# Norms' 1/sqrt chains moved from GpSimd to VectorE, with squares and normalised rows made in halves

## The chip, the core and the metric

The kernel runs on one core of one Trainium2 chip. The metric is the device time of one execution in microseconds (us). TensorE (PE) multiplies matrices, VectorE (DVE) and ScalarE (ACT) do elementwise work, GpSimd (POOL) did the small chains that the change is about, and SyncE (SP) issues the DMAs. Each engine works through its own queue in order; engines wait for one another at semaphores.

## The reference

Two layers, each of three sub-layers on `x` of 256 rows by 1024 columns, in float32:

```python
for l in range(DEPTH):
    x = x + 0.5 * gate(0) * _swiglu(norm_mod(x, 0), w_ffn_up[l, 0], w_ffn_down[l, 0])
    x = x + gate(1) * _mixer(norm_mod(x, 1), w_in[l], ...)
    x = x + 0.5 * gate(2) * _swiglu(norm_mod(x, 2), w_ffn_up[l, 1], w_ffn_down[l, 1])
```

`norm_mod` divides each row by the root of its mean square (plus 1e-6), scales it by `g_norm * (1 + scale)` and adds `shift`. Shift, scale and gate come from the condition vector `c` through the large matrix `w_ada`. `_swiglu` is an FFN of width 2816. The mixer projects the rows once and runs an RG-LRU, a stick-breaking attention and a forgetting attention on parts of the columns. Each part's output is divided by its own root mean square before the last projection.

## The kernel before

The rows lie in two tiles of 128, `x0` and `x1` (index `t`), which stay in SBUF. All weights stream through a ring of six buffers (`raw`, 512 KB each). Each weight tile is split into two float32r parts: ScalarE casts it to `H` (L248), VectorE subtracts to get `L` (L249), and TensorE makes three products (rows' high part with `H` and with `L`, rows' low part with `H`). The `w_ada` tiles come through the same ring and are read by VectorE alone (L290 for shift and scale, L313 for the gates).

Between two sub-layers stands a norm, once for each row tile. There are five such boundaries: **B1** first FFN to first mixer, **B2** first mixer to its second FFN, **B3** from layer 1 to layer 2, **B4** first FFN of layer 2 to its mixer, **B5** that mixer to the last FFN. At each, for `x0` and then for `x1`:

- `residual` (L441, L442, VectorE) adds the gated result to `x`, half by half.
- `norm_sq` (ScalarE, `junk`) squares the row and sums it into `ss`. Before, one instruction did it, except for `x1` after an FFN, where two halves were added up on GpSimd (L397, `v`).
- `rsqrt` finds the inverse root by an integer guess and two Newton steps: `ny` (L356), `na` (L360), `ny` (L361), `na`, `ny`, five dependent instructions on 128x1. They ran on GpSimd.
- `norm_xn` (L404, ScalarE) scales the row into `xn`.
- `norm_out` transposes `xn` on TensorE (L415, `tp`), applies scale and shift (`hf`, half on ScalarE L423, half on VectorE L425), and splits into `hTh` (L428, L430) and `hTl` (L431), which the next sub-layer's matmuls read.

While `x1`'s chain runs, TensorE works on the next sub-layer with `x0`: 48 matmuls of 512 columns. The mixer has the same `rsqrt` on 128x2 in `group` for its two attention outputs (`f` and `s`), between `gj` (L842) and `yn` (L848), whose transposes are `ty` (L850). The output projection's matmuls are `wo`. At the very start the two norms (L918) have their squares on VectorE; of their chains, that of `x0` ran on GpSimd and that of `x1` on VectorE. GpSimd otherwise only clears the gates' accumulators (`acc`, L308).

The tile framework decides where each instruction stands in its engine's queue: it follows estimates of when operands will be there, and the explicit limits in the code (`tc.issue_after`, `pending`). So an operation that moves to another engine also changes what stands around it.

Of the kernel before, what the change touches and what calls it, by code (L numbers as in the profile page):

```python
# [12 lines left out]
I32 = mybir.dt.int32  # L13
AF = mybir.ActivationFunctionType
ALU = mybir.AluOpType
# [4 lines left out]
D = 1024  # L20
# [6 lines left out]
EPS = 1e-6  # L27
# [67 lines left out]
def trunk_kernel(ctx: ExitStack, tc: tile.TileContext, x, c, wst, ada, par, cst, row, bgate, wg, out):  # L95
    nc = tc.nc
# [13 lines left out]
    def W4(shape, dt=F32, name="w4"):  # L110
        return w4.tile(shape, dt, tag="w4", name=name)

    def W2(shape, dt=F32, name="w2"):
        return w2.tile(shape, dt, tag="w2", name=name)

    def SM(shape, dt=F32, name="sm"):
        return sm.tile(shape, dt, tag="sm", name=name)
# [4 lines left out]
    def PD(shape, name):  # L122
        return psd.tile(shape, F32, tag="d", name=name)

    def PT(shape, name):
        return pst.tile(shape, F32, tag="t", name=name)

    V, A, T, S = nc.vector, nc.scalar, nc.tensor, nc.sync
# [4 lines left out]
    xt = [x_t[:, 0:D] for x_t in xe]  # L133
# [34 lines left out]
    def R(name):  # L168
        o, n = ROW[name]
        return r_sb[:, o:o + n]  # L170
# [8 lines left out]
    for n in range(2):  # L179
        q = slice(n * 512, (n + 1) * 512)  # L180
# [71 lines left out]
    def unit(key):  # L252
        if key not in live:
            raw = rawp.tile([128, 1024], F32, tag="raw", name="raw")
            S.dma_start(out=raw, in_=wst[W_UNITS[key]])
            live[key] = split(raw)
        return live[key]

    def mm3(o, xh, xl, wh, wl, first, last):
        T.matmul(o, lhsT=xh, rhs=wh, start=first, stop=False)  # L260
        T.matmul(o, lhsT=xh, rhs=wl, start=False, stop=False)  # L261
        return T.matmul(o, lhsT=xl, rhs=wh, start=False, stop=last)  # L262
# [87 lines left out]
            ada_step(1)  # L350


    def rsqrt(v, n, name, E=nc.gpsimd):
        y = SM([128, n], name=name + "y")
        a = SM([128, n], name=name + "a")
        E.tensor_scalar(out=y.bitcast(I32), in0=v.bitcast(I32), scalar1=-0.5, scalar2=float(0x5F1FFFF9),  # L356
                        op0=ALU.mult, op1=ALU.add)
        for c in (-2.38924456, -3.0 / NEWTON ** 2):
            if n == 1:
                E.tensor_scalar(out=a, in0=y, scalar1=v, scalar2=y, op0=ALU.mult, op1=ALU.mult)  # L360
                E.tensor_scalar(out=y, in0=a, scalar1=c, scalar2=y, op0=ALU.add, op1=ALU.mult)  # L361
            else:
                E.tensor_tensor(out=a, in0=y, in1=y, op=ALU.mult)
                E.tensor_tensor(out=a, in0=a, in1=v, op=ALU.mult)
                E.tensor_scalar(out=a, in0=a, scalar1=c, scalar2=None, op0=ALU.add)
                E.tensor_tensor(out=y, in0=a, in1=y, op=ALU.mult)
        return y


# [12 lines left out]
    xn_t, r_t = {}, {}  # L382

    def norm_in(t):
        norm_sq(t)
        norm_xn(t)

    def norm_sq(t, parts=1):
        n = D // parts
        ss = SM([128, parts], name="ss")  # L390
        for i in range(parts):
            q = slice(i * n, (i + 1) * n + i // (parts - 1) if parts > 1 else D + 1)
            junk = W2([128, D + 1], BF16, name="junk")
            A.activation(junk[:, q], xe[t][:, q], AF.Square, scale=1.0 / 32, accum_out=ss[:, i:i + 1])
        if parts == 2:
            v = SM([128, 1], name="v")
            nc.gpsimd.tensor_tensor(out=v, in0=ss[:, 0:1], in1=ss[:, 1:2], op=ALU.add)  # L397
        else:
            v = ss
        r_t[t] = rsqrt(v, 1, "n")  # L400

    def norm_xn(t):
        xn_t[t] = W4([128, D], name="xn")
        A.activation(xn_t[t], xt[t], AF.Copy, scale=r_t[t])  # L404

    def norm_out(l, j, t):
        ada_until(ada_ss, (l, j, KT - 1, 1))
# [27 lines left out]
    def residual(l, j, t, o, each=lambda t, q: None):  # L435
        ada_until(ada_gate, (l, j, KT - 1))
        g = gate_t[l, j]
        for n in range(2):
            q = slice(n * 512, (n + 1) * 512)
            tmp = W2([128, 512], name="tmp")  # L440
            V.tensor_tensor(out=tmp, in0=o[n], in1=g[:, q], op=ALU.mult)  # L441
            V.tensor_tensor(out=xt[t][:, q], in0=xt[t][:, q], in1=tmp, op=ALU.add)  # L442
            each(t, q)
        if t == NT - 1:
            gate_free[j % 2] = True
# [24 lines left out]
    def ffn(l, s, after, pre={}):  # L470
# [66 lines left out]
        def down(j, t):  # L537
            if j == 0:
                dn[t] = [PD([128, 512], name="dn") for _ in range(2)]
            w = [unit(("dn", l, s, j, i)) for i in range(2)]  # L540

            order = [(i, n) for i in range(2) for n in range(2)]
            for i, n in sorted(order, key=lambda p: p[1]) if j == NCH - 1 else order:
                q = slice(n * 512, (n + 1) * 512)
                mm3(dn[t][n], *gT[j, i, t], w[i][0][:, q], w[i][1][:, q],
                    j == 0 and i == 0, j == NCH - 1 and i == 1)
            if j == NCH - 1:
                if after is None:
                    residual(l, j3, t, dn[t], lambda t, q: S.dma_start(out=out[t * 128:(t + 1) * 128, q], in_=xt[t][:, q]))
                    return  # L550
                residual(l, j3, t, dn[t])
                norm_sq(t, 1 + t)
                if t == 1:
                    norm_xn(1)
                    pending.append(lambda: after[1](1))
# [11 lines left out]
        a, b = NCH - 2, NCH - 1  # L567
# [14 lines left out]
    def mixer(l, after):  # L582
# [41 lines left out]
        if True:  # L624
            for f2, hf in enumerate(halves):
                for f in (2 * f2, 2 * f2 + 1):
                    A.activation(u[:, f, :], xT[:, f, 3:3 + SEQ], AF.Identity,
                                 scale=cw[:, 3 * 4 + f:3 * 4 + f + 1], bias=cbias[:, f:f + 1])
                    for tap in (2, 1, 0):
                        V.scalar_tensor_tensor(out=u[:, f, :], in0=xT[:, f, tap:tap + SEQ],  # L630
                                               scalar=cw[:, tap * 4 + f:tap * 4 + f + 1], in1=u[:, f, :],
                                               op0=ALU.mult, op1=ALU.add)
# [13 lines left out]
        for t in range(NT):  # L646
            o = proj(FX, t)
            if t == 1:
# [8 lines left out]
                for t in range(NT):  # L657
# [14 lines left out]
                            in1=r8.unsqueeze(2).to_broadcast([128, 8, HD]), op=ALU.mult)  # L672
            for i in range(2):
                V.tensor_tensor(out=qa[t][:, 4 * i:4 * i + 4, 0:HD], in0=qa[t][:, 4 * i:4 * i + 4, 0:HD],
                                in1=R(f"gqk{l}")[:, i * HD:(i + 1) * HD].unsqueeze(1).to_broadcast([128, 4, HD]),
                                op=ALU.mult)
# [29 lines left out]
        for f2, hf in enumerate(halves):  # L706
# [7 lines left out]
            for f in (2 * f2, 2 * f2 + 1):  # L714
                V.tensor_tensor_scan(out=hs[:, f, :], data0=rg[:, f, :], data1=ig[:, f, :], initial=0.0,
                                     op0=ALU.mult, op1=ALU.add)
# [87 lines left out]
        def split(f0, n, src):  # L804
            for i in range(n):
                g = gm[:, f0 + i:f0 + i + 1]
                yh, yl = hTh[:, :, f0 + i, :], hTl[:, :, f0 + i, :]
                y = src[:, i, :].rearrange("p (t q) -> p t q", t=NT)
                A.activation(yh, y, AF.Copy, scale=g)
                V.scalar_tensor_tensor(out=yl, in0=y, scalar=g, in1=yh.bitcast(F32),  # L810
                                       op0=ALU.mult, op1=ALU.subtract)


        for t in range(NT):
# [3 lines left out]
            q = slice(t * 128, (t + 1) * 128)  # L818
# [19 lines left out]
        def group(name, f0, src):  # L838
            s2g = SM([128, 2], name="gs" + name)
            junk = W2([128, 256], name="gj")  # L840
            for t in range(NT):
                A.activation(junk, src[t], AF.Square, accum_out=s2g[:, t:t + 1])  # L842
            nc.gpsimd.tensor_scalar(out=s2g, in0=s2g, scalar1=1.0 / 256, scalar2=EPS, op0=ALU.mult, op1=ALU.add)
            rs = rsqrt(s2g, 2, "g" + name)
            yn = W2([128, 2, 256], name="yn")
            tp = PT([128, 2, SEQ], name="ty")
            for t in range(NT):
                V.tensor_scalar(out=yn[:, t, :], in0=src[t], scalar1=rs[:, t:t + 1], scalar2=RS, op0=ALU.mult, op1=ALU.mult)  # L848
                for i in range(2):
                    T.transpose(tp[:, i, t * 128:(t + 1) * 128], yn[:, t, i * 128:(i + 1) * 128], ident)  # L850
            split(f0, 2, tp)
# [5 lines left out]
        def values(y, products):  # L857

            with ExitStack() as behind:
                for i, (t, h, w, v) in enumerate(products):  # L860
                    mul = T.matmul(y[:, t, h, :], lhsT=w, rhs=v, start=i == 0, stop=True, skip_group_check=True)
                    if i == 0:
# [8 lines left out]
                        in1=rin.unsqueeze(2).to_broadcast([128, 8, HD]), op=ALU.mult)  # L871
# [36 lines left out]
    def norm(l, j):  # L908
        return norm_in, lambda t: norm_out(l, j, t)
# [4 lines left out]
    for t in range(NT):  # L914
        ss = SM([128, 1], name="ss")
        junk = W2([128, D + 1], BF16, name="junk")
        x1 = xe[t][:, 0:D + 1]
        V.scalar_tensor_tensor(out=junk, in0=x1, scalar=1.0 / D, in1=x1, op0=ALU.mult, op1=ALU.mult, accum_out=ss)  # L918
        r_t[t] = rsqrt(ss, 1, "n", V if t == 1 else nc.gpsimd)
        norm_xn(t)  # L920
    xnT = [W4([128, NT, 4, 128], name="xnT") for _ in range(2)]
    for g in range(2):
# [7 lines left out]
    for k in range(KT):  # L930
        for v in range(2):
# [3 lines left out]
                        scalar2=S_t[0, 0][:, k:k + 1], op0=ALU.mult, op1=ALU.add)  # L935
# [117 lines left out]
```

## Time and profile before

| | us |
|---|---|
| median of three runs | 1032.69 (1031.07 to 1036.15) |
| the profiled execution | 1031.17 |
| its span, first to last instruction | 1029.4 |
| VectorE busy | 759.9 (74%) |
| ScalarE busy | 538.1 (52%) |
| GpSimd busy | 53.3 (5%), 108 instructions |

The page gives the busy time of each engine, then the chain of work that ended last, followed back from the last instruction, then the costliest groups. The trace behind it gives the instructions in order of time: start, duration, engine, line, `out<-in`, shapes, and in square brackets how long the engine had been idle and what ended that. Ends of matmuls are modelled, and one that overlaps the next shows a longer duration than its spacing: back-to-back 512-column matmuls start 0.23 us apart at the full clock.

### The profile page before, as it was taken

What the parts mean: (1) busy time and instruction counts of PE and PEld (TensorE: products, weight loads), DVE (VectorE), ACT (ScalarE), POOL (GpSimd) and SP (SyncE); (2) the same over time, 40 slices, a digit from 0 to 9 for tenths busy, and PEclk for the clock granted to TensorE, in tenths of its full rate; (3) what the DMA queues carried; (4) which work ended last, traced back from release to release, by engine and by line L of the source; (5) the groups of instructions that cost most, each with busy time, mean ns of one, the idle gap of its engine ahead of it and who ended that gap; (6) DMA issues with size and microseconds to landing.
All of it is one profiled execution on the core that took longest, in us unless ns stands there. A gap on an engine that the chain in (4) does not pass through costs nothing.

```text
span 1029.4 us, 15807 instructions
## 1 busy us (share of the span) xinstructions
PE 994.3 (97%) x6038; PEld 871.8 (85%) x6038; DVE 759.9 (74%) x1107; ACT 538.1 (52%) x855; POOL 53.3 (5%) x108
## 2 busy tenths in 40 slices
PE   5999999989999899999999999999999989999998
PEld 4999999868787799999878999997777778999996
DVE  7988978769786898888569888665677559745452
ACT  5373534458774444354454455455679454635340
POOL 1000000120011200000020000001100120000000
PEclk9999999989999999999999999999999999999999
DMA  8989998757473699999539999853542328755511
GB/s 307 362 308 315 332 332 312 268 207 255 155 252 117 241 362 336 335 331 328 194 124 340 342 334 335 304 191 137 173 175 83 103 86 324 266 203 171 198 63 41
DMA packets 68922, 248.10 MB, mean 241 GB/s; under 512 B 7783, under 2 KB 8423, under 8 KB 68846
## 3 DMA queue, kind: packets, MB, share of 16 engines
q1 hardware_dynamic: 68846, 247.10, 68.2%
q8 instruction: 47, 0.77, 0.3%
q14 instruction: 29, 0.24, 0.1%
HBM read 246.02 MB, written 1.05 MB: 240 GB/s over the span
## 4 chain that ended last, share of the span: by engine, by line
PE 83%; ACT 6%; POOL 4%; DVE 3%; issue 2%; DMA 1%; SPq 0%; DVEq 0%; POOLq 0%; ACTq 0%
PE up L467 38%; PE dn L260 8%; PE dn L262 8%; PE dn L261 8%; PE up L271 5%; PE pj L271 5%; PE up L273 3%; PE pj L273 2%; ACT H L248 2%; POOL na L360 1%; PE wo L260 1%; PE wo L261 1%; PE wo L262 1%; POOL ny L361 1%; PE tp L415 1%
## 5 line engine op out<-in xcount | busy, mean ns | idle before, releaser
L249 DVE TENSOR_TENSOR L<-raw,H 128x1024 fp32r<-128x1024 f32 x320 | 380.5, 1221 | 72.6 <-ACT H L248 71.8
L248 ACT CAST H<-raw 128x1024 fp32r<-128x1024 f32 x320 | 328.1, 1051 | 84.5 <-PE up L467 35.0
L467 PE MATMUL up<-hTh,H 128*128 128x256 f32 x1088 | 211.0, 282 | 3.7 <-ACT H L248 3.7
L467 PE MATMUL up<-hTl,H 128*128 128x256 f32 x1088 | 211.9, 283 | 0.0
L467 PE MATMUL up<-hTh,L 128*128 128x256 f32 x1088 | 211.3, 282 | 0.0
L467 PEld LDWEIGHTS up<-hTh,H 128*128 128x128 f32 x1088 | 169.2, 189 | 9.9 <-ACT H L248 4.1
L467 PEld LDWEIGHTS up<-hTl,H 128*128 128x128 f32 x1088 | 165.1, 189 | 0.0
L467 PEld LDWEIGHTS up<-hTh,L 128*128 128x128 f32 x1088 | 164.4, 189 | 0.0
L459 ACT ACTIVATE sg<-up 128x256 f32<-128x256 f32 x88 | 33.7, 383 | 223.9 <-PE up L467 183.6
L260 PE MATMUL dn<-H,gh 128*128 128x512 f32 x352 | 141.1, 401 | 1.6 <-ACT gh L532 1.6
L262 PE MATMUL dn<-H,gl 128*128 128x512 f32 x352 | 140.0, 399 | 0.0
L261 PE MATMUL dn<-L,gh 128*128 128x512 f32 x352 | 139.7, 397 | 0.0
L290 DVE SCALAR_TENSOR_TENSOR raw<-raw,cb 128x1024 f32<-128x1024 f32 x96 | 114.0, 1220 | 2.1 <-DMA raw<-in_ada 2.1
L262 PEld LDWEIGHTS dn<-H,gl 128*128 128x128 f32 x352 | 66.6, 189 | 15.8 <-DVE gl L533 0.5
L260 PEld LDWEIGHTS dn<-H,gh 128*128 128x128 f32 x352 | 66.7, 189 | 15.2 <-ACT gh L532 3.0
L261 PEld LDWEIGHTS dn<-L,gh 128*128 128x128 f32 x352 | 66.9, 190 | 12.8
L516 DVE TENSOR_TENSOR sg<-sg,up 128x256 f32<-128x256 f32 x68 | 28.5, 419 | 66.0 <-ACT sg L459 65.7
L271 PE MATMUL pj<-H,hTh 128*128 128x512 f32 x160 | 66.2, 414 | 0.0
L273 PE MATMUL pj<-H,hTl 128*128 128x512 f32 x160 | 65.9, 412 | 0.0
L271 PE MATMUL up<-H,hTh 128*128 128x512 f32 x160 | 64.2, 401 | 0.4 <-DVE hTh L428 0.4
L271 PE MATMUL pj<-L,hTh 128*128 128x512 f32 x160 | 64.5, 403 | 0.0
L271 PE MATMUL up<-L,hTh 128*128 128x512 f32 x160 | 63.1, 395 | 0.0
(249 smaller groups left out, 1101.5 us busy)
## 6 DMA issues: line engine op xcount, KB each, us to landing
raw<-in_wst SPq DMA_DIRECT2D x320, 512.0 KB, 5.2
raw<-in_ada SPq DMA_DIRECT2D x144, 512.0 KB, 5.3
x<-in_x SPq DMA_DIRECT2D x2, 512.0 KB, 3.7
wgt<-in_wg SPq DMA_DIRECT2D x2, 512.0 KB
out_x<-x SPq DMA_DIRECT2D x4, 256.0 KB
once<-in_cst SPq DMA_DIRECT2D x1, 192.0 KB
p_sb<-in_par SPq DMA_DIRECT2D x1, 148.0 KB, 5.4
r_sb<-in_row SPq DMA_DIRECT2D x1, 132.0 KB, 6.1
```

Source lines behind the costliest of these rows:

```text
L248: A.copy(h, raw)
L249: V.tensor_tensor(out=lo, in0=raw, in1=h.bitcast(F32), op=ALU.subtract)
L260: T.matmul(o, lhsT=xh, rhs=wh, start=first, stop=False)
L261: T.matmul(o, lhsT=xh, rhs=wl, start=False, stop=False)
L262: return T.matmul(o, lhsT=xl, rhs=wh, start=False, stop=last)
L271: T.matmul(o, lhsT=hh[:, k, :], rhs=part, start=k == 0 and i == 0, stop=False)
L273: mul = T.matmul(o, lhsT=hl[:, k, :], rhs=w(k)[0], start=False, stop=k == KT - 1)
L290: V.scalar_tensor_tensor(out=raw, in0=raw, scalar=1.0, in1=cb, op0=ALU.mult, op1=ALU.mult, accum_out=st[:, v, k:k + 1])
L360: E.tensor_scalar(out=a, in0=y, scalar1=v, scalar2=y, op0=ALU.mult, op1=ALU.mult)
L459: used.append(A.activation(*a, **k))
L467: return T.matmul(o[:, v], lhsT=w[:, q:q + 128], rhs=(hTh, hTl)[h][:, :, k, :], start=opens, stop=True, skip_group_check=True)
L516: V.tensor_tensor(out=sg, in0=sg, in1=o[:, 1], op=ALU.mult)
```

## The change

All `rsqrt` chains run on VectorE, as do the sum of the two halves' squares (`v`) and the scaling ahead of the mixer's chains (L843). For 128x2 the last two of four operations of a Newton step are one `scalar_tensor_tensor`. Squares are always made in two halves (512 and 513 columns), and `xn` in two halves of 512. Lines 394 and 397 are now 393 and 396.

```diff
-    def rsqrt(v, n, name, E=nc.gpsimd):
+    def rsqrt(v, n, name):
...
-        E.tensor_scalar(out=y.bitcast(I32), in0=v.bitcast(I32), scalar1=-0.5, scalar2=float(0x5F1FFFF9),
+        V.tensor_scalar(out=y.bitcast(I32), in0=v.bitcast(I32), scalar1=-0.5, scalar2=float(0x5F1FFFF9),
                         op0=ALU.mult, op1=ALU.add)
         for c in (-2.38924456, -3.0 / NEWTON ** 2):
             if n == 1:
-                E.tensor_scalar(out=a, in0=y, scalar1=v, scalar2=y, op0=ALU.mult, op1=ALU.mult)
-                E.tensor_scalar(out=y, in0=a, scalar1=c, scalar2=y, op0=ALU.add, op1=ALU.mult)
+                V.tensor_scalar(out=a, in0=y, scalar1=v, scalar2=y, op0=ALU.mult, op1=ALU.mult)
+                V.tensor_scalar(out=y, in0=a, scalar1=c, scalar2=y, op0=ALU.add, op1=ALU.mult)
             else:
-                E.tensor_tensor(out=a, in0=y, in1=y, op=ALU.mult)
-                E.tensor_tensor(out=a, in0=a, in1=v, op=ALU.mult)
-                E.tensor_scalar(out=a, in0=a, scalar1=c, scalar2=None, op0=ALU.add)
-                E.tensor_tensor(out=y, in0=a, in1=y, op=ALU.mult)
+                V.tensor_tensor(out=a, in0=y, in1=y, op=ALU.mult)
+                V.tensor_tensor(out=a, in0=a, in1=v, op=ALU.mult)
+                V.scalar_tensor_tensor(out=y, in0=a, scalar=c, in1=y, op0=ALU.add, op1=ALU.mult)
...
     def norm_in(t):
-        norm_sq(t)
+        norm_sq(t, 2)
...
-            nc.gpsimd.tensor_tensor(out=v, in0=ss[:, 0:1], in1=ss[:, 1:2], op=ALU.add)
+            V.tensor_tensor(out=v, in0=ss[:, 0:1], in1=ss[:, 1:2], op=ALU.add)
...
-        A.activation(xn_t[t], xt[t], AF.Copy, scale=r_t[t])
+        for q in (slice(0, D // 2), slice(D // 2, D)):
+            A.activation(xn_t[t][:, q], xt[t][:, q], AF.Copy, scale=r_t[t])
...
-                norm_sq(t, 1 + t)
+                norm_sq(t, 2)
...
-            nc.gpsimd.tensor_scalar(out=s2g, in0=s2g, scalar1=1.0 / 256, scalar2=EPS, op0=ALU.mult, op1=ALU.add)
+            V.tensor_scalar(out=s2g, in0=s2g, scalar1=1.0 / 256, scalar2=EPS, op0=ALU.mult, op1=ALU.add)
...
-        r_t[t] = rsqrt(ss, 1, "n", V if t == 1 else nc.gpsimd)
+        r_t[t] = rsqrt(ss, 1, "n")
```

The queues around the moved instructions differ at every boundary. At B1, ScalarE's queue from `x0`'s squares (`x_88`) to its normalised row, where L248 is the weight cast, L459 the SiLU of the last up-projection and L532 a cast that the down-projection waits for; before:

```order
L248 CAST H<-raw 128x1024 x2
L394 ACTIVATE junk,ss<-x_88 128x1025
L248 CAST H<-raw 128x1024
L459 ACTIVATE sg<-up 128x256
L404 ACTIVATE xn<-x_88,ny 128x1024
L454 ACT_TABLE_LOAD
L532 CAST gh<-tg 128x256
```

and now:

```order
L248 CAST H<-raw 128x1024
L393 ACTIVATE junk,ss<-x_88 128x512
L393 ACTIVATE junk,ss<-x_88 128x513
L248 CAST H<-raw 128x1024 x2
L459 ACTIVATE sg<-up 128x256
L454 ACT_TABLE_LOAD
L404 ACTIVATE xn<-x_88,ny 128x512 x2
L532 CAST gh<-tg 128x256
```

The squares stand one weight cast earlier, and the table load stands ahead of the normalised row, no longer between it and `gh`.

VectorE's queue at B1 from the end of `x1`'s residual (`x_89`) on, before:

```order
L442 TENSOR_TENSOR x_89<-x_89,tmp 128x512 x2
L249 TENSOR_TENSOR L<-raw,H 128x1024 x3
L604 MEMSET xT 128x4x3
L249 TENSOR_TENSOR L<-raw,H 128x1024 x2
L425 TENSOR_SCALAR hf<-tp,G_1351,S_1352 128x128 x3
L428 CAST hTh<-hf 128x512
```

and now:

```order
L249 TENSOR_TENSOR L<-raw,H 128x1024
L396 TENSOR_TENSOR v<-ss 128x1
L249 TENSOR_TENSOR L<-raw,H 128x1024
L356 TENSOR_SCALAR ny<-v 128x1
L313 SCALAR_TENSOR_TENSOR acc<-raw,cs,acc 128x1024
L360 TENSOR_SCALAR na<-ny,v 128x1
L249 TENSOR_TENSOR L<-raw,H 128x1024
L361 TENSOR_SCALAR ny<-na,ny 128x1
L249 TENSOR_TENSOR L<-raw,H 128x1024
L360 TENSOR_SCALAR na<-ny,v 128x1
L249 TENSOR_TENSOR L<-raw,H 128x1024
L361 TENSOR_SCALAR ny<-na,ny 128x1
```

The chain's steps now alternate with the five weight subtractions that used to stand together, and one L313 has moved up among them. On TensorE the transposes of `x1` have moved down at all five boundaries, by 9, 9, 14, 5 and 9 matmuls.

In the first mixer, VectorE's queue from the forgetting attention's output (`yf`) to its normalised form (`yn`), before:

```order
L870 TENSOR_TENSOR yf<-yfx,rin 128x512
L290 SCALAR_TENSOR_TENSOR raw,ss_2710<-raw,cb 128x1024 x3
L848 TENSOR_SCALAR yn<-yf,gfy 128x256 x2
L290 SCALAR_TENSOR_TENSOR raw,ss_2710<-raw,cb 128x1024
L810 SCALAR_TENSOR_TENSOR hTl<-ty,p_sb,hTh 128x2x128
```

and now, from the fourth L290 behind `yf` (three more with `gsf` and `gfy` between them stand ahead of this piece):

```order
L290 SCALAR_TENSOR_TENSOR raw,ss_2718<-raw,cb 128x1024
L363 TENSOR_TENSOR gfa<-gfy 128x2
L295 TENSOR_TENSOR S_2720<-ss_2718,p_sb 128x8
L300 SCALAR_TENSOR_TENSOR G_2719<-ss_2718,p_sb 128x8
L364 TENSOR_TENSOR gfa<-gfa,gsf 128x2
L249 TENSOR_TENSOR L<-raw,H 128x1024
L365 SCALAR_TENSOR_TENSOR gfy<-gfa,gfy 128x2
L302 SCALAR_TENSOR_TENSOR G_2719<-G_2719,p_sb 128x8
L249 TENSOR_TENSOR L<-raw,H 128x1024
L363 TENSOR_TENSOR gfa<-gfy 128x2
L249 TENSOR_TENSOR L<-raw,H 128x1024
L364 TENSOR_TENSOR gfa<-gfa,gsf 128x2
```

Four L290 and three L249 now stand between `yf` and `yn`, where there were three L290. TensorE's queue has 36 output-projection matmuls (L260 to L262) ahead of the `ty` of this group, where it had 21. In the second mixer the chain stands behind two L249, as before, and its steps follow one another.

## The prediction

> **What bounds the kernel now.** I read the page first: the busy times of the engines, then the engines' shares of the chain that ended last.
>
> ```profile
> PE 994.3 (97%) x6038; PEld 871.8 (85%) x6038; DVE 759.9 (74%) x1107; ACT 538.1 (52%) x855; POOL 53.3 (5%) x108
> PE 83%; ACT 6%; POOL 4%; DVE 3%; issue 2%; DMA 1%; SPq 0%; DVEq 0%; POOLq 0%; ACTq 0%
> ```
>
> TensorE works for 97% of the span and no matmul goes away. The 4% of GpSimd in the chain (some 41 us) are not what can be won: behind most of them TensorE has other work that it must do anyway. So I went to the list of waits, and took from it those of TensorE on which a norm stands:
>
> ```profile
> PE tp L415 <- ACT xn L404: 13.0, 6, 2.6
> ...
> PE up L467 <- ACT H L248: 3.7, 1, 3.7
> ...
> PE ty L850 <- DVE yn L848: 3.1, 3, 1.4
> ...
> PE tp L927 <- ACT xn L404: 2.2, 2, 1.4
> ...
> PE dn L260 <- ACT gh L532: 1.6, 2, 1.0
> ```
>
> The columns are the total in us, the number of waits, and the longest. Together they are 23.6 us. That is the most that shorter chains can return, but for the clock, which follows at B1. Then I asked for the groups of instructions that write the chain's tiles, and for the longest step in the order of time (shortest, median and longest in ns).
>
> ```profile
> L361 POOL TENSOR_SCALAR ny<-na,ny x22: 264/264/2313, 6.6 to 843.0; 128x1 f32<-128x1 f32 x22
> L360 POOL TENSOR_SCALAR na<-ny,v x6: 340/340/3318, 221.1 to 727.1; 128x1 f32<-128x1 f32 x6
> L361 DVE TENSOR_SCALAR ny<-na,ny x2: 163/187/211, 9.8 to 10.3; 128x1 f32<-128x1 f32 x2
> ```
>
> A step takes 0.26 to 0.34 us on GpSimd, and ten times that at worst. It takes about 0.2 on VectorE. What an inserted step costs VectorE, and a half row costs ScalarE, is in these rows, the first two from the start and the last from B1:
>
> ```profile
> 14.01 0.16 DVE L295 TENSOR_TENSOR S<-ss,p_sb 128x1 f32<-128x1 f32 x1
> 14.08 1.22 DVE L290 SCALAR_TENSOR_TENSOR raw<-raw,cb 128x1024 f32<-128x1024 f32 x1
> 218.14 0.63 ACT L394 ACTIVATE junk<-x 128x512 bf16<-128x512 f32 x1 [0.47 <-DVE x L442]
> ```
>
> A 128x1 step delays the next large instruction by 0.07 (start to start) to 0.2 (its own duration). I take 0.14, the middle. [...]
>
> **B1, `x0`.** This is the largest term. The rows in order of time, and one window with TensorE's granted clock (the third number from the end):
>
> ```profile
> 207.24 1.15 ACT L404 ACTIVATE xn<-x,ny 128x1024 f32<-128x1024 f32 x1 [3.51 <-POOL ny L361]
> 208.40 1.28 ACT L454 ACT_TABLE_LOAD   x1
> 208.44 1.11 PE L415 MATMUL tp<-c_sb,xn 128*128 128x128 f32 x4 [2.31 <-ACT xn L404]
> 210.12 0.80 PE L260 MATMUL dn<-H,gh 128*128 128x512 f32 x1 [0.57 <-ACT gh L532]
> 215.66 0.39 PE L271 MATMUL pj<-H,hTh 128*128 128x512 f32 x1
> 215.90 0.39 PE L271 MATMUL pj<-L,hTh 128*128 128x512 f32 x1
> ...
> 209.00:212.00 3.00, 2.43 (x8) 1.54 (x7) 1.62 (x2) 2.99 (x7) 0.00 (x0) 0.50 0.50 198
> ```
>
> TensorE runs dry at 208.44 - 2.31 = 206.13. Until the first `pj` at 215.66 pass 9.53 us, in which it does 12 matmuls of 512 columns (12 x 0.23 = 2.8) and 8 transposes (0.8). So 5.9 are lost: the gaps of 2.31 and 0.57, and about 3.0 because the work behind them runs at half the clock. ScalarE stood idle for 3.51 ahead of `xn`; afterwards the squares stand one cast (1.05) earlier, the five steps cost about 1 us plus one L249, and the table load of 1.28 falls into the idle time instead of between `xn` and `gh`. I get `ny` near 204.9, the load done by 205.4, the halves of `xn` at 205.4 and 206.0, and `gh` at 206.9 instead of 210.1. The first transposes then follow TensorE's last matmul directly, and about 0.4 us of waiting for `gh` stays. With that the clock should hold. **-5.0** of the 5.9; bounds -5.6 (nothing left but fractions) and -1 (the load runs late, a gap near 1.5 us stays and the clock falls all the same).
>
> **B1, `x1`.** Here the chain is placed among weight work.
>
> ```profile
> 218.56 4.63 DVE L249 TENSOR_TENSOR L<-raw,H 128x1024 fp32r<-128x1024 f32 x4
> 221.07 3.32 POOL L360 TENSOR_SCALAR na<-ny,v 128x1 f32<-128x1 f32 x1
> 225.59 1.15 ACT L404 ACTIVATE xn<-x,ny 128x1024 f32<-128x1024 f32 x1 [6.11 <-POOL ny L361]
> 226.79 1.10 PE L415 MATMUL tp<-c_sb,xn 128*128 128x128 f32 x8 [1.92 <-ACT xn L404]
> ```
>
> The L249 take 4.63 / 4 = 1.16 each, and while they run a GpSimd step lasts 3.32. Now five L249 (5.8), one L313 (about the same 1.16) and six steps (6 x 0.14 = 0.84) stand in line from 218.56: 7.8, so the last `ny` ends near 226.4, 0.8 later than before. What was an interference becomes a queue of the same length. The first half of `xn` saves 0.5 (0.63 against 1.15). The nine matmuls that now go ahead of the transposes (9 x 0.23 = 2.1) fill the gap of 1.92, but stand no longer behind it, where they covered `hf` and `hTh`; and one more L290 (1.22) stands ahead of the last `hTl`. 0.8 - 0.5 and a little of that: **+0.5**; bounds -0.5 (the halves alone) and +1.5 (all of the L290).
>
> **B2 and B5, `x1`.** The two are alike; rows of B2:
>
> ```profile
> 334.15 2.35 DVE L249 TENSOR_TENSOR L<-raw,H 128x1024 fp32r<-128x1024 f32 x2
> 341.11 1.15 ACT L404 ACTIVATE xn<-x,ny 128x1024 f32<-128x1024 f32 x1 [3.53 <-POOL ny L361]
> 342.31 1.09 PE L415 MATMUL tp<-c_sb,xn 128*128 128x128 f32 x8 [2.60 <-ACT xn L404]
> 344.60 0.43 DVE L428 CAST hTh<-hf 128x512 fp32r<-128x512 f32 x1
> 343.00:346.00 3.00, 3.00 (x17) 2.48 (x16) 2.44 (x7) 1.97 (x6) 0.00 (x0) 1.00 0.84 262
> ```
>
> From 334.15, five L249 (5.8), one 128x256 product (0.3) and six steps (0.84) give 341.1, and 0.2 for the last step's own length: 341.3, against 341.11. The halves return 0.5, so `hTh`, 3.92 us after `xn` began (344.60 + 0.43 - 341.11), comes 0.3 earlier. The gap of 2.60 is filled with nine matmuls, but those are the ones that TensorE did while `hTh` was made; the first matmul of `x1` follows `hTh`. **-0.3 each**; bounds -2.1 (the nine matmuls are pure gain) and +1.0 (VectorE one L249 later).
>
> **B3, `x1`, and B4.** The wait at B3, and those of B4 with a window behind the second:
>
> ```profile
> 532.83 1.09 PE L415 MATMUL tp<-c_sb,xn 128*128 128x128 f32 x8 [1.64 <-ACT xn L404]
> 714.36 0.50 PE L260 MATMUL dn<-H,gh 128*128 128x512 f32 x1 [1.03 <-ACT gh L532]
> 729.02 1.09 PE L415 MATMUL tp<-c_sb,xn 128*128 128x128 f32 x8 [1.92 <-ACT xn L404]
> 731.00:734.00 3.00, 3.00 (x9) 2.38 (x8) 2.24 (x5) 1.18 (x3) 0.00 (x0) 0.55 0.20 79
> ```
>
> At B3 fourteen matmuls (3.2 us) go ahead of the transposes and cover the whole 1.64; by the same sum as at B1 the chain itself ends about 1.5 later, less 0.5 for the halves, so I count half of the gap: **-0.8** (-1.6 to +0.5). At B4 for `x0` the table load again moves ahead, and 1.03 becomes about 0.6: **-0.4** (-1.0 to +0.5). At B4 for `x1` only four L249 stand among the steps, so `ny` comes no later than before; five matmuls (1.2) and the halves (0.5) shrink the gap of 1.92 to 0.2, and the window after it, 3 us at a clock of 0.55, then costs 3 x 0.45 = 1.35 less. That would be 3.0; the five matmuls are missing behind the transposes, which takes back 0.8: **-2.2** (-3.0 to 0).
>
> **The mixers' groups.** The first mixer's end, with a window in which VectorE's share is the third busy time, then the second mixer:
>
> ```profile
> 290.00:300.00 10.00, 9.30 (x49) 7.71 (x47) 10.00 (x15) 8.08 (x15) 0.00 (x0) 1.00 0.67 214
> 302.20 0.69 DVE L870 TENSOR_TENSOR yf<-yfx,rin 128x512 f32<-128x512 f32 x1 [0.37 <-PE yfx L861]
> 308.68 0.62 DVE L848 TENSOR_SCALAR yn<-yf,gfy 128x256 f32<-128x256 f32 x2 [2.35 <-POOL gfy L366]
> 313.04 0.44 PE L850 MATMUL ty<-c_sb,yn 128*128 128x128 f32 x2 [1.37 <-DVE yn L848]
> ...
> 810.50 0.70 PE L850 MATMUL ty<-c_sb,yn 128*128 128x128 f32 x4 [0.95 <-DVE yn L848]
> 813.59 0.44 PE L850 MATMUL ty<-c_sb,yn 128*128 128x128 f32 x2 [0.78 <-DVE yn L848]
> ```
>
> In the first, `yn` began 5.8 us after `yf` ended (308.68 - 302.89). Now four L290, three L249 (7 x 1.16 = 8.1) and some eleven small steps (1.5) stand between: 9.6, so 3.8 later. TensorE has fifteen matmuls more ahead (3.5) and its gap of 1.37 in hand, but fifteen fewer behind. **+1.0**; bounds -1.4 (the gap goes) and +3.8 (no cover). In the second, the ten steps follow one another at 0.2 against 0.3 and more, which takes away most of 0.95 + 0.78: **-1.4** (-1.7 to 0).
>
> **The start.** The first up-projection waits 3.7 for ScalarE. One L290 (1.22) fewer stands ahead of the first `hf`, while five steps cost VectorE 0.7: **-0.5** (-1.2 to +1.1, all five steps at their full 0.2 on the path with nothing gained).
>
> **The sum**: -0.5 - 5.0 + 0.5 + 1.0 - 0.6 - 0.8 - 0.4 - 2.2 - 1.4 = -9.4. Against the profiled execution's 1031.17 that is **1021.8**. That execution is 1.5 below the median of the three runs, so against the median 1023.3 would be as fair; I keep 1021.8. GpSimd's and SyncE's queues lose or gain nothing that TensorE waits for: no DMA is added.
>
> **Rivals.**
>
> *VectorE becomes the bound at the places where it is full.* For: 10.00 of 10 us busy just before the first mixer's `yf`, and small steps in line behind 1.16 us instructions. Then the group costs +4 instead of +1, B1's `x1` +1.5 instead of +0.5, and B2 and B5 together +0.7 instead of -0.6: -9.4 + 3.0 + 1.0 + 1.3 = -4.1, **1027.1**. Against: fifteen more matmuls now stand ahead of the group's transposes.
>
> *The chain is held up by a weight cast, and the kernel gets slower.* A step behind an L249 in the queue also waits for what that L249 waits for, the cast on ScalarE:
>
> ```profile
> 797.77 1.23 DVE L249 TENSOR_TENSOR L<-raw,H 128x1024 fp32r<-128x1024 f32 x1 [2.41 <-ACT H L248]
> ```
>
> One such wait in each of the five `x1` chains is 5 x 2.41 = 12.05, and TensorE then runs dry at each: -9.4 + 12.0 = +2.6, **1033.8**. It decides from four such waits on. Against: at B1 the L249 ran without a break.
>
> *The half clock does not depend on the gaps.* At B2 a gap of 2.60 was followed by the full clock (1.00), at B1 one of 2.31 by 0.50. If the slow stretches come as before, 3.0 of B1 and 1.35 of B4 are not won: **1026.2**. The Trainium skill, "TensorE: Matmul & The Clock Gate", section "HAM oscillation — how this bites in real kernels", speaks for this rival: only idle gaps over about 3.4 us should bring the clock down, and 2.31 is less; the trace disagrees in so far as the clock fell behind gaps of 2.31 and 1.92.
>
> **Chances and range.** The forecast 0.58, the full VectorE 0.20, the held-up chain 0.10, the clock 0.08, and 0.04 for more than the forecast. The group, B2, B3 and B5 share one unknown (steps queued among large ones), so their bounds add up: 2.4 + 1.8 + 1.8 + 0.8 = 6.8 below the sum, which is 1015.0. Above, the range takes in both faster rivals and ends at the slower one: **1015 to 1034**. About 0.5% (5.2 us) is what a measurement of this kernel can tell from no change. The forecast nearly always gains more than that, the first and third rivals a little less, and the second loses less than that unless more waits come: faster 0.62, same 0.31, slower 0.07.
>
> **What would show it.** In the changed kernel's trace: no GpSimd work but the clears; `xn` at B1 for `x0` begun with under 2 us of idle time ahead, the table load ahead of it, and a clock of 1.00 in the 9 us behind; TensorE's waits for `tp` shrunk from 13.0 to under 4, with waits for `hTh` or `hTl` of `x1` in their stead at the five sites; `ny` of `x1` later at B1, B2, B3 and not at B4; `yn` of the first mixer some 9 to 10 us behind `yf`. I am wrong if the clock falls at B1 again, if L249 in a chain show waits for casts, or if `ty` waits over 3 us in the first mixer.

## The result and the profile after

| | us |
|---|---|
| before, median of four runs | 1033.09 (1031.07 to 1036.15) |
| changed, median of four runs | 1022.80 (1020.06 to 1025.10) |
| ratio, 95% interval | 0.9897 (0.9858 to 0.9935) |
| span of the profiled execution, before and changed | 1029.4 and 1022.7 |

The change made the kernel 10 us faster. The forecast was 1021.8. The profiled execution of the changed kernel took 1024.51 us, so the two profiles stand only 6.7 apart; why executions of one program differ by so much is part of what follows. One of the twelve runs of the kernel with halves alone (below) took 1088.93 us at a mean clock of 0.849, and its ratio is formed without it.

The changed kernel's page, its busy times and the shares of the chain that ended last:

```profile
PE 996.9 (97%) x6038; PEld 872.7 (85%) x6038; DVE 773.9 (76%) x1204; ACT 543.0 (53%) x881; POOL 5.8 (1%) x10
PE 89%; ACT 5%; DVE 4%; DMA 1%; issue 1%; DVEq 0%; ACTq 0%
```

GpSimd keeps its clears only. Its 4% are gone from the chain, and DVE has 1% more. Four of TensorE's waits, from the changed kernel's list (total, number, longest; the last is the first up-projection's, at the start):

```profile
PE tg L529 <- ACT hf L423: 3.1, 3, 1.0
PE tx L612 <- ACT lxt L609: 2.7, 2, 1.9
PE tp L415 <- ACT xn L404: 1.9, 3, 1.3
PE up L467 <- ACT H L248: 1.9, 1, 1.9
```

The waits for `xn` fell from 13.0 to 1.9, those for `yn` are gone. In their place stand 3.1 and 2.7 that were not in the list before: TensorE has passed the transposes of `x1` (`tp`) and waits a little further on, at the next instruction that stands ahead of `x1`'s first matmul (`tg`, `tx`).

The largest term, B1 for `x0`, in the changed kernel's order of time:

```profile
202.66 1.28 ACT L454 ACT_TABLE_LOAD   x1
203.96 1.34 ACT L404 ACTIVATE xn<-x,ny 128x512 f32<-128x512 f32 x2
205.08 0.60 PE L415 MATMUL tp<-c_sb,xn 128*128 128x128 f32 x4
205.20 0.35 ACT L532 CAST gh<-tg 128x256 fp32r<-128x256 f32 x1
208.94 0.39 PE L271 MATMUL pj<-H,hTh 128*128 128x512 f32 x1
```

The load lies ahead of `xn`, neither `xn` nor `gh` nor the first `tp` has a wait in brackets, and the mixer's first matmul came 3.86 us behind the first `tp`, where it had been 7.22 and a gap of 2.31 ahead of that. Now B1 for `x1`, its chain on VectorE and what TensorE does behind it, with a window whose third number from the end is the granted clock:

```profile
213.87 1.22 DVE L249 TENSOR_TENSOR L<-raw,H 128x1024 fp32r<-128x1024 f32 x1
215.00 0.15 DVE L396 TENSOR_TENSOR v<-ss 128x1 f32<-128x1 f32 x1
215.07 1.22 DVE L249 TENSOR_TENSOR L<-raw,H 128x1024 fp32r<-128x1024 f32 x1
216.21 0.14 DVE L356 TENSOR_SCALAR ny<-v 128x1 int32<-128x1 int32 x1
...
221.36 0.20 DVE L361 TENSOR_SCALAR ny<-na,ny 128x1 f32<-128x1 f32 x1
221.59 1.34 ACT L404 ACTIVATE xn<-x,ny 128x512 f32<-128x512 f32 x2 [6.78 <-DVE ny L361]
222.37 1.27 PE L415 MATMUL tp<-c_sb,xn 128*128 128x128 f32 x8 [1.26 <-ACT xn L404]
225.59 1.12 PE L612 MATMUL tx<-c_sb,lxt 128*128 128x128 f32 x4 [1.95 <-ACT lxt L609]
226.35 0.78 PE L271 MATMUL pj<-H,hTh 128*128 128x512 f32 x1
224.00:231.00 7.00, 5.41 (x15) 4.46 (x16) 3.10 (x8) 3.79 (x7) 0.00 (x0) 0.52 0.73 290
```

Six steps of about 0.2 us lasted from 215.00 to 221.56, since one long instruction stands between each two. TensorE lost 1.26 and 1.95, and from 224.2 to 231.1 it had half the clock. This place gave back much of what `x0` had won 10 us earlier.

The move did not make `x1`'s chain shorter. From its first step (`v` where there is one) to its last it took 6.0, 4.8, 4.1, 4.9 and 4.8 us at the five boundaries on GpSimd, and takes 6.6, 5.7, 5.7, 4.5 and 5.7 on VectorE. `x0`'s chain, which has less weight work among its steps, fell from 4.6 to 2.8 at B1.

### The profile page after: what moved, and what is told of

The parts are those of the page before. It is cut to its first block, busy times and chain, and to the rows that moved or that the text cites. A ratio compares the mean times of both kernels' runs of the same rounds, so it can differ in the third digit from the quotient of the medians.

```text
span 1022.7 us, 15837 instructions
## 1 busy us (share of the span) xinstructions
PE 996.9 (97%) x6038; PEld 872.7 (85%) x6038; DVE 773.9 (76%) x1204; ACT 543.0 (53%) x881; POOL 5.8 (1%) x10
## 4 chain that ended last, share of the span: by engine, by line
PE 89%; ACT 5%; DVE 4%; DMA 1%; issue 1%; DVEq 0%; ACTq 0%
PE up L467 38%; PE dn L262 8%; PE dn L260 8%; PE dn L261 8%; PE up L271 6%; PE pj L271 6%; PE pj L273 3%; PE up L273 3%; DVE L L249 1%; PE wo L260 1%; PE wo L262 1%; PE wo L261 1%; ACT H L248 1%; ACT hf L423 1%; PE go L637 1%
## 5 line engine op out<-in xcount | busy, mean ns | idle before, releaser
L249 DVE TENSOR_TENSOR L<-raw,H 128x1024 fp32r<-128x1024 f32 x320 | 382.1, 1221 | 78.0 <-ACT H L248 77.1
L248 ACT CAST H<-raw 128x1024 fp32r<-128x1024 f32 x320 | 327.6, 1052 | 98.8 <-DMA raw<-in_wst 44.0
L459 ACT ACTIVATE sg<-up 128x256 f32<-128x256 f32 x88 | 33.8, 384 | 203.6 <-PE up L467 167.0
L260 PE MATMUL dn<-H,gh 128*128 128x512 f32 x352 | 140.2, 398 | 0.2 <-ACT gh L532 0.2
L262 PE MATMUL dn<-H,gl 128*128 128x512 f32 x352 | 139.6, 397 | 0.0
L290 DVE SCALAR_TENSOR_TENSOR raw<-raw,cb 128x1024 f32<-128x1024 f32 x96 | 114.3, 1219 | 0.6 <-DMA raw<-in_ada 0.6
L262 PEld LDWEIGHTS dn<-H,gl 128*128 128x128 f32 x352 | 66.1, 188 | 15.7 <-DVE gl L533 0.5
L260 PEld LDWEIGHTS dn<-H,gh 128*128 128x128 f32 x352 | 66.1, 188 | 13.5 <-ACT gh L532 1.4
```

What stands on the lines that cost most here:

```text
L248: A.copy(h, raw)
L249: V.tensor_tensor(out=lo, in0=raw, in1=h.bitcast(F32), op=ALU.subtract)
L290: V.scalar_tensor_tensor(out=raw, in0=raw, scalar=1.0, in1=cb, op0=ALU.mult, op1=ALU.mult, accum_out=st[:, v, k:k + 1])
L459: used.append(A.activation(*a, **k))
```

## The experiments

Ratios are against the kernel before, run on the same chip beside each group: median 1032.53 for the first four, 1033.70 for the next four, 1033.03 for the last three. I also compared where TensorE stands at the same matmul in two traces: how much earlier or later a stage starts, less the same for the stage before, is what a place gave. The table has these differences in us against the trace of before (negative is faster). The mark between B1 (or B4) for `x1` and the mixer behind it is the mixer's 66th `pj` matmul. The expectations quote a reading at the mixer's first `go`, where B1 for `x1` came out as +3.9 and +2.8. That mark misleads: three `pg` matmuls stand ahead of it in the kernel before and none in the changed one, so some 0.9 us of the difference is order and not time.

| place | forecast | changed | changed again | x0 only | x1 only | contiguous |
|---|---|---|---|---|---|---|
| start | -0.5 | -0.9 | -2.3 | -1.7 | -0.8 | -2.2 |
| B1, x0 | -5.0 | -5.8 | -5.9 | -5.9 | -0.4 | -5.8 |
| B1, x1 | +0.5 | +4.8 | +3.7 | +4.4 | +0.3 | -1.7 |
| first mixer up to wo | 0 | +1.2 | +0.8 | +0.5 | +1.0 | -0.7 |
| its groups and end | +1.0 | -0.6 | -0.6 | +0.3 | +0.4 | 0.0 |
| B2, x1 | -0.3 | +0.9 | -0.7 | 0.0 | -0.7 | -2.0 |
| B3, x1 | -0.8 | -0.3 | -0.3 | 0.0 | -0.3 | -1.8 |
| B4, x0 | -0.4 | -0.5 | -0.5 | -0.5 | 0.0 | -0.5 |
| B4, x1 | -2.2 | -2.7 | -2.7 | -1.5 | -2.2 | -3.4 |
| second mixer, groups | -1.4 | -2.1 | -2.1 | +0.1 | -0.2 | -2.1 |
| B5, x1 | -0.3 | -0.7 | -0.7 | +1.6 | -0.7 | -2.0 |
| sum | -9.4 | -6.7 | -11.3 | -2.6 | -3.6 | -22.2 |

**The chains without the halves.** All chains on VectorE, rows and squares whole as before:

```diff
...
-        for q in (slice(0, D // 2), slice(D // 2, D)):
-            A.activation(xn_t[t][:, q], xt[t][:, q], AF.Copy, scale=r_t[t])
+        A.activation(xn_t[t], xt[t], AF.Copy, scale=r_t[t])
...
```

> Leaves out the halves: squares and normalised rows are made as before, only the 1/sqrt chains are on VectorE. Theory A (the chains' place is what counts, above all at B1 for x0, where 6.7 us of waiting and half clock went): most of the gain of 10 us stays, 1024 to 1026 us, each x1 site about 0.5 us later than in the full change. Theory B (the halves are what counts, since the first transposes start after half a row): most of the gain is gone, 1029 to 1031 us.

Measured 1026.84 us, ratio 0.9934 (0.9917 to 0.9952): the chains alone bring 0.7%, in a time a little above theory A's range and well under B's. At B1 for `x0` the order is already the better one, in this kernel's rows:

```profile
206.17 1.16 ACT L403 ACTIVATE xn<-x,ny 128x1024 f32<-128x1024 f32 x1 [0.20 <-DVE ny L361]
210.39 0.50 PE L271 MATMUL pj<-H,hTh 128*128 128x512 f32 x1 [0.88 <-DVE hTh L427]
```

`xn` comes 2.2 us later than with the halves, though two halves cost ScalarE more (1.34) than the whole row (1.16), and 0.88 us of waiting for `hTh` stays. By the trace B1 for `x0` gave 3.9 here and 5.8 with the halves. The medians are 4 us apart, but the two intervals overlap a little, so it is this place that shows what the halves add.

**The halves without the move.** The kernel before with squares and rows in halves (the edit above, the other way, on the kernel before).

> Leaves out the move: the chains stay on GpSimd as before, only squares and normalised rows are made in halves. Theory A: little gain, 1030 to 1032 us, waits of TensorE for xn at B1 still over 2 us. Theory B: most of the gain, 1024 to 1026 us.

1031.18 us, ratio 0.9987 (0.9973 to 1.0001): no change that could be told. TensorE's wait for `xn` at B1 for `x0` is as it was (2.31), and that for `gh` is longer (it was 0.57):

```profile
207.93 0.66 PE L416 MATMUL tp<-c_sb,xn 128*128 128x128 f32 x4 [2.27 <-ACT xn L405]
210.23 0.50 PE L260 MATMUL dn<-H,gh 128*128 128x512 f32 x1 [1.64 <-ACT gh L533]
```

`x0`'s chain began 1.7 us earlier than before (200.89 against 202.60), but on GpSimd it now took 6.2 us instead of 4.6 and ended where it had (207.12 against 207.20). So theory A holds: here the halves gained only together with chains that were no longer late by themselves.

**The changed kernel again.** No edit.

> The changed kernel once more, to see whether its two stretches at half clock (224 to 231 us behind gaps of 1.26 and 1.95 us, 344 to 347 us behind one of 1.04) belong to the program. Theory C (a gap of TensorE brings the clock down): the same stretches at the same places, the time within 1 us of 1022.8. Theory D (the clock's window runs freely, and a gap is only an occasion): other places or another number of stretches in this execution, each worth 2 to 3 us, and times spread over 1019 to 1026 us.

1022.82 us, ratio 0.9906 (0.9886 to 0.9926), runs from 1019.90 to 1026.64. The gaps were the same to 0.1 us, the clock was not. The stretch at B1 came in both profiles, but in this one it was half as long:

```profile
224.00:230.00 6.00, 5.96 (x21) 4.84 (x22) 2.81 (x4) 2.84 (x4) 0.00 (x0) 0.72 0.71 283
```

That is (1 - 0.72) x 6 = 1.7 us of full speed lost, against (1 - 0.52) x 7 = 3.4 in the first. The wait at B2 and the window behind it, first in the first profile of the changed kernel, then in this one:

```profile
342.91 0.44 PE L529 MATMUL tg<-c_sb,sg 128*128 128x128 f32 x2 [1.04 <-ACT hf L423]
344.00:347.00 3.00, 3.00 (x9) 2.35 (x8) 2.96 (x5) 0.89 (x2) 0.00 (x0) 0.50 0.42 169
```

```profile
339.91 0.44 PE L529 MATMUL tg<-c_sb,sg 128*128 128x128 f32 x2 [1.04 <-ACT hf L423]
342.00:346.00 4.00, 4.00 (x19) 3.26 (x18) 3.93 (x5) 1.05 (x1) 0.00 (x0) 1.00 0.40 156
```

The same gap of 1.04 was followed by half the clock once and by the full clock once. Theory D holds in this form: the stretches come close to gaps, but the program does not settle whether a gap brings one. The Trainium skill, page "TensorE: Matmul & The Clock Gate", section "What's actually happening", says that the window over which activity is judged is free-running. These two traces are in line with that, but they do not show the window itself.

**The chain contiguous.** At the five `x1` sites the subtractions that stood among the steps are put behind the last step; the first 7, 5, 5, 8 and 5 of the next sub-layer may go ahead, and the five after them are held:

```diff
+    chain, skips = {}, [7, 5, 5, 8, 5]
...
-        V.tensor_tensor(out=lo, in0=raw, in1=h.bitcast(F32), op=ALU.subtract)
+        with tc.issue_after(chain["step"].ins) if 0 <= chain.get("n", -1) < 5 else nullcontext():
+            V.tensor_tensor(out=lo, in0=raw, in1=h.bitcast(F32), op=ALU.subtract)
+        if chain:
+            chain["n"] += 1
...
+            chain.update(step=step, n=-n)
...
```

> The changed kernel, but at the five x1 sites the weight subtractions that stood between the chain's steps come behind its last step, so that the chain takes about 1.2 us and not 6. Theory E (the new waits behind x1's transposes, 1.26 + 1.95 + 1.04 + 0.99 + 0.77 + 1.05 = 7.1 us with the half clock behind them, come from the queue among the subtractions): those waits go, 1012 to 1016 us. Rival F (the subtractions were urgent for x0's matmuls, or hf and hTh set the end anyway): TensorE waits for L at the same places instead, 1021 to 1026 us.

1010.30 us, ratio 0.9780 (0.9764 to 0.9796): 12.5 us under the changed kernel, somewhat more than theory E gave. VectorE and TensorE at B1 in this kernel:

```profile
213.28 0.15 DVE L400 TENSOR_TENSOR v<-ss 128x1 f32<-128x1 f32 x1
213.35 1.28 DVE L317 SCALAR_TENSOR_TENSOR acc<-raw,cs,acc 128x1024 f32<-128x1024 f32 x1
214.55 0.15 DVE L360 TENSOR_SCALAR ny<-v 128x1 int32<-128x1 int32 x1
214.73 0.27 DVE L364 TENSOR_SCALAR na<-ny,v 128x1 f32<-128x1 f32 x1
...
215.60 0.21 DVE L365 TENSOR_SCALAR ny<-na,ny 128x1 f32<-128x1 f32 x1
217.14 1.03 PE L422 MATMUL tp<-c_sb,xn 128*128 128x128 f32 x8
```

From `v` to the last `ny` pass 2.5 us (1.2 of it one L317 that was not held), no longer 6.5. The transposes find `xn` there and have no wait. The trace shows no half clock until the output is written; of the four runs none took over 1010.55 us. The chains take 2.5, 1.8, 1.5, 1.5 and 1.8 us at the five boundaries.

The edit moved something else as well: the transposes of `x1` stand behind 39, 39, 33, 39 and 39 matmuls of the next sub-layer again, as before the change. So the nine (at B3 fourteen, at B4 five) that had moved ahead of them can cover `hf` and `hTh` once more. How the 12.5 us divide between the short chain and this order, no run here separates.

**Only x0, and only x1.** The change at the five boundaries for one row tile each; the other tile, the groups and the start's chains as before (at the start, too, the chosen tile's `xn` comes in halves):

```diff
...
+    NEW = {0: True, 1: False}
...
+        r_t[t] = rsqrt(v, 1, "n", V if NEW[t] else nc.gpsimd)
...
```

> Only x0's norms at the five boundaries as in the change (chain on VectorE, halves); x1's, the mixers' groups and the start as before. By the places in the traces, B1 for x0 gave 5.8 us and B4 for x0 0.5. If these terms add up, 1026 to 1027 us, and B1 shows no wait for xn of x0. If the gain at B1 is taken back behind it (x1's chain on GpSimd, the clock falling at the next gap), 1029 to 1032.

> Only x1's norms at the five boundaries as in the change, the rest as before. By the places in the two traces of the changed kernel, the five sites sum to between +1.5 us (B1 +3.9, B2 +0.9, B3 -0.3, B4 -2.4, B5 -0.6) and -1.2: 1031 to 1034 us, no gain. If the move is good for x1 by itself, and what it lost at B1 came from x0's earlier end, 1027 to 1029.

Only `x0`: 1029.78 us, ratio 0.9964 (0.9945 to 0.9982), the second alternative. B1 for `x0` gave its 5.9, but `x1`'s wait grew from 1.92 to 3.99, because TensorE arrives earlier and GpSimd's chain among the subtractions is no shorter (6.9 us, 6.0 before):

```profile
215.44 3.38 POOL L360 TENSOR_SCALAR na<-ny,v 128x1 f32<-128x1 f32 x1
222.09 1.09 PE L420 MATMUL tp<-c_sb,xn 128*128 128x128 f32 x8 [3.99 <-ACT xn L409]
```

Only `x1`: 1028.35 us, ratio 0.9942 (0.9919 to 0.9964), again not what the sum of the places gave but the second alternative. With `x0` as before, `x1` is about even at B1 (+0.3) and gains at the other four boundaries; the wait of 1.92 for `xn` became one of about the same length, further on:

```profile
229.16 0.65 PE L617 MATMUL tx<-c_sb,lxt 128*128 128x128 f32 x4 [2.01 <-ACT lxt L614]
```

So the +4.8 and +3.7 of the changed kernel at B1 for `x1` are not a cost of the chain on VectorE: with `x1` on GpSimd it was +4.4. They are `x0`'s gain, which ends at the next chain.

**The groups' chains back on GpSimd**, all else as changed (two calls in `group`).

> The change without its part in the mixers: the two groups' chains stay on GpSimd. By the traces the second mixer's group gave 2.2 us and the first about 0.6: 1025 to 1026 us, with TensorE waiting for yn again (1.37, 0.95, 0.78). If the queue on VectorE had cost in the first mixer what it gave in the second, 1022 to 1023.

1025.66 us, ratio 0.9912 (0.9878 to 0.9946). The median is in the first alternative, but against the changed kernel's 0.9906 and 0.9897 no difference can be told by time. TensorE's waits for `yn` in the second mixer are back in part:

```profile
807.04 0.70 PE L855 MATMUL ty<-c_sb,yn 128*128 128x128 f32 x4 [0.73 <-DVE yn L853]
810.15 0.83 PE L855 MATMUL ty<-c_sb,yn 128*128 128x128 f32 x4 [0.55 <-DVE yn L853]
299.00:302.00 3.00, 3.00 (x16) 3.00 (x15) 2.35 (x4) 2.23 (x6) 0.49 (x1) 0.50 0.10 37
```

The second mixer's group is worth about 2 us by the traces. For the first one this profile is no witness: the clock was at a half from 296.5 to 306.8 (a window inside this is the last line).

**Contiguous, but whole rows and squares** (the first edit on the contiguous kernel).

> The contiguous chains, without the halves. The chains on VectorE without halves took 4 us more than with them (1026.84 against 1022.82). If a half saves only where TensorE waits for the row, and the contiguous chain took those waits away, 1010 to 1011.5 us. If the halves matter by themselves, 1013 to 1015.

1013.23 us, ratio 0.9805 (0.9771 to 0.9839): the second alternative by its median, 3 us above the contiguous kernel, though the intervals of the two overlap. Its profile shows 0.96 us of waiting at B1 for `x0` and 1.1 each at B2 and B5 for `L`, where the contiguous kernel had none and 0.55:

```profile
210.10 0.50 PE L275 MATMUL pj<-H,hTh 128*128 128x512 f32 x1 [0.96 <-DVE hTh L434]
332.63 0.50 PE L275 MATMUL up<-L,hTh 128*128 128x512 f32 x1 [1.11 <-DVE L L251]
```

By the traces B1 for `x0` gave 3.9 here and 5.8 with the halves, and B2 0.2 and 2.0. At these places the halves keep their worth.

**Contiguous, but x1's chains on GpSimd.** VectorE's subtractions wait behind a one-column copy of `ny`:

```diff
...
+        r_t[t], step = rsqrt(v, 1, "n", nc.gpsimd if t == 1 else V)
+        if t == 1:
+            step = V.tensor_copy(SM([128, 1], name="seen"), r_t[t])
...
```

> As the contiguous kernel, but x1's chains back on GpSimd; VectorE's subtractions wait behind a one-column copy of ny, so that nothing runs beside the chain. Theory G (not the engine counts but that no weight work stands in or beside the chain): the steps take 0.26 to 0.34 us again, six of them under 2.5 us with the handovers, against 1.2 on VectorE; most stays hidden behind x0's matmuls, 1011 to 1015 us, no step over 1.3 us. Theory H (GpSimd's steps are slow by themselves at these places): steps of 2 to 3 us appear again and the time goes back to 1020 and more.

1016.58 us, ratio 0.9846 (0.9819 to 0.9873), against 1009.86 for the contiguous kernel beside it. GpSimd's steps at B1 (the first beside an L317), and TensorE's wait behind them:

```profile
214.00 1.10 POOL L360 TENSOR_SCALAR ny<-v 128x1 int32<-128x1 int32 x1
215.20 0.34 POOL L364 TENSOR_SCALAR na<-ny,v 128x1 f32<-128x1 f32 x1
215.64 0.27 POOL L365 TENSOR_SCALAR ny<-na,ny 128x1 f32<-128x1 f32 x1
221.85 0.50 PE L275 MATMUL pj<-H,hTh 128*128 128x512 f32 x1 [0.95 <-DVE hTh L436]
```

Theory G is right about the steps: none but the first is over 0.35 us. The time is 1.6 above its range. Its profiled run took 1013.19 with a mean clock of 0.999, the other three 1016.19 to 1017.45 with 0.994 and 0.995. The chain takes 3.1 us at B1 and 2.1 to 2.2 elsewhere, 0.3 to 0.7 more than on VectorE, and gaps of about 1 us are back, of the kind that were followed by half clocks above. By the medians about half of what this order won over the changed kernel (6 of 12.5 to 13 us) is to be had on either engine; VectorE is worth some 7 us more. That the slower three runs lost their time to half clocks is likely from their mean clock, but only the fastest run was profiled.

**One more subtraction ahead at B2 and B5, and the contiguous kernel again**: 7, 6, 5, 8 and 6 subtractions, and no edit.

> As the contiguous kernel, with one more subtraction let ahead of the chain at B2 and B5, where TensorE waited 0.55 us for L each. If these waits cost what they show, 1.1 us less than the contiguous kernel beside it; if the chain's end then comes too late, the waits reappear at the transposes and nothing is won.

> The contiguous kernel once more beside the two: 1009 to 1011 us, and no stretch at half clock, as in its first profile.

1008.66 us, ratio 0.9766 (0.9743 to 0.9790), beside 1009.86, ratio 0.9779 (0.9756 to 0.9801). The profile has no wait for `L` at B2 and B5 any more and the size (1.2 us by the medians) is the forecast one, but the intervals overlap. It has the lowest median here, 2.3% under the kernel before. The contiguous kernel came out as expected again, with no stretch at half clock.

## Why the prediction was right, point by point

- **B1, x0: right.** -5.0 was forecast; -5.8 and -5.9 in the two traces. `xn` and the load ahead of it came in the order that the sum assumed, about 1.4 us earlier than it (203.96 instead of 205.4), the clock held for `x0`, and even the wait for `gh`, priced at 0.4, did not occur.
- **B1, x1: the wrong term.** The chain's length was right (7.6 us from the end of `x1`'s residual, 213.95, to the last `ny`, 221.56; forecast 7.8). The price of +0.5 was not. It compared the chain's end with that of before and counted `x0`'s 5 us as won apart from it. But TensorE arrived 6.7 us earlier, and `x1`'s residual only 4.7. And the nine matmuls that moved ahead of the transposes were taken as "a little"; they were the cover for `hf` and `hTh`, and 1.95 us of waiting stand there instead. The dearest part was not in the sum at all: the half clock cost 3.4 us in one profile and 1.7 in the other. The waits grew by 1.3 (1.26 + 1.95 against 1.92), and one of 0.5 for `x0`'s own second `hTh` came ahead of them. "I am wrong if the clock falls at B1 again" did come true, for `x1`. The experiment with `x0` alone shows the first part: 5.9 won, 4.4 given back.
- **B2, B3, B5: about right**, once the half clock behind B2 in one of two executions is set aside: -0.7, -0.3, -0.7 against -0.3, -0.8, -0.3. The mechanism was nearly as said: the wait for `xn` became one of 1.0 us, though for `hf` (ahead of `tg`) and not for `hTh`.
- **B4: right**, -0.5 and -2.7 against -0.4 and -2.2.
- **The groups.** The second gave -2.1 (forecast -1.4). In the first, `yn` came 8.95 us behind `yf` (302.14 to 311.09; forecast 9.6), but the fifteen matmuls covered it: -0.6 instead of +1.0. Not forecast is the mixer's inside, up to the first `wo`: +1.2 and +0.8. It is not there in the contiguous kernel, and +1.0 in the one with `x1` alone. Most of it is TensorE waiting longer for ScalarE: for `vt` (L833) 1.15 us instead of 0.69, for `gh` (L790) 0.4 instead of 0.2, for `sbt` (L759) 0.3 where no wait was listed. What makes ScalarE late I did not find; VectorE is busy for 10.00 of 10 us ahead of `wo` in both kernels.
- **The rivals.** The full VectorE did not decide: the groups came out better than its price. No subtraction among a chain's steps waited for its cast, so the slower case did not occur. The third was half right: the stretch at B1 for `x0` did go, and so did that at B4, but another came at B1 for `x1`, in both profiles of the changed kernel.
- **The sum** -9.4 lies between the traces' -6.7 and -11.3, and the medians are 10.3 apart. That is partly good fortune: in the first trace `x0` at B1, the groups and the start gave 3.5 us more than forecast and `x1` at B1 and the mixer's inside 5.5 less, in the second 5.1 more and 4.0 less.

## What to carry to other kernels

A chain of small dependent steps is as long as what the scheduler puts between them: six steps of 0.2 us took 6.5 among long instructions and 2.5 nearly in a row. The edit that brought them together, and the transposes back to their old place, was worth more here (12.5 us) than the choice of the engine (some 7 us in that order). When a wait is taken away, reckon the next one anew from the new arrival time of the engine that waited, and count each instruction that moved ahead of a wait as missing behind it.

## What the hardware showed that was not expected

- Half clock is not a property of the program alone. In 17 runs of the kernel before, the mean granted clock ran from 0.987 to 0.996 and the time from 1038.15 to 1030.07; the five runs at 0.996 took 1030.07 to 1032.42, and the one at 0.987 took 1038.15. The contiguous kernel and the one with one more subtraction ahead, which have no gap of a microsecond behind the start, had a clock of 0.998 to 1.000 in all twelve runs and a small spread (1009.28 to 1010.55 for the eight runs of the first).
- Shorter gaps than I had thought of go with it: 1.04 us at B2 in one execution. In the thirteen profiles every stretch at half clock between the first 25 us and the last 3 began during a gap of at least 1 us or within 2.4 us of its end, while gaps of 2.60 at B2 and B5 in the kernel before had none. By the clock records of the traces each such stretch lasted 3.41 us or two or three times that (6.83, 10.24).
- GpSimd's 128x1 step (`na`) took 3.32 and 3.38 us beside VectorE's subtractions, which last 1.16 each, and 0.34 with none beside it.
